# A decoder trunk whose order of instructions a planner makes: other planning rates, another order of two matmul groups, one scaling and two stores on other engines

## The chip, the cores and the metric

The kernel runs on one core of a Trainium2 chip. The metric is the time of one execution on the device in microseconds (us), lower is better. The core has five engines with queues of their own: TensorE (PE, with its weight loads shown apart as PEld), VectorE (DVE), ScalarE (ACT), GpSimd (POOL) and SyncE (SP, which only starts transfers). ACT and POOL can start transfers too. An engine works through its queue in order and waits at an instruction until its semaphores are reached.

## The reference, cut to what matters

Two decoder layers over 512 tokens of width 1024, 16 heads of 64, in float32.

```python
h = x
for layer in range(2):
    hn = rms_norm(h, attn_norm[layer])
    if layer == 0:   # mixer A: window 128, learned sinks, T5 bias
        h = h + swa_sink_mixer(hn, ...)
    else:            # mixer B: compressed, selected and windowed keys, gated
        h = h + nsa_mixer(hn, ...)
    h = h + swiglu(rms_norm(h, ffn_norm[layer]), w_gu[layer], w_down[layer])
return rms_norm(h, final_norm)
```

In mixer A each head's row of exponentials is divided by its sum (which includes the sink) before it meets the values: `p = e / (sum(e) + exp(sink - m))`. The feed-forward part is `(silu(gate) * up) @ w_down` with an inner width of 2816.

## The kernel before, in words

**Precision.** Every float32 operand is held as two halves, a rounded high part and the rest as a low part, so a product is three matmuls: high weight by high and by low data, low weight by high data (`step3`, line 614). The halves of weights are made on the chip from the loaded `raw` tile: either ACT rounds and DVE subtracts (`halves`), or, in `halves_by_dma` (line 589), one engine writes the negated rounded weights to `wlo` and a POOL transfer adds the weights from memory to it. With `aside=True` POOL does the rounding itself.

**Stages, with their times in the profile.** Loads, first norm and the keys and values of layer 0 (0 to about 25 us); attention A (to about 113); output projection A (to about 160); the plain part of feed-forward 0 (to about 239); its seven-product part (`seven`, line 1058, a Strassen-like scheme over 256 columns, to 480); the last down projection; projections of layer 1 (520 to 580); attention B (580 to 740); output projection B; feed-forward 1 in the same form (seven products from 860 to 1098); last down projection, final norm and stores.

**What sets the order.** The code does not issue instructions as it stands. Each call is recorded (`method`, line 202; `add`, line 210) with a cost and, for a transfer, a number of bytes and an extra delay `late`. Because the recorded calls are made from one lambda, nearly every instruction in the profile stands on line 207, and the tiles' names tell what it is. `issue` (line 274) then plans all engines together: for each of three pairs of transfer rate and latency in `SPEEDS` (line 58) it makes 6 rounds; in each, `plan` (line 423) is a list scheduler that gives an order, `latest` (line 311) works backwards from its end and gives each instruction a due time for the next round, and `replay` (line 360) plays that order 6 times with costs raised at random by up to 5% on all engines but PE and with the rates of `SPEEDS` in turn. The order with the lowest mean over the replays is issued. Every engine's queue is fixed by it, and so is the tile buffer that each instruction gets.

**The places that the change touches.**
- Small loads on ACT: `gains` (line 713), `rel_table` into `tab` (line 720) and two pieces of `onehot` into `oh` (line 725). In `add` a transfer that ACT starts has `late` 900.
- `project` (line 625) issues the 16 matmuls with the high weights first and the 8 with the low weights last. `query_job` (line 885) and `out_first_half` (line 892) use `mm3` (line 621), which takes the three of each slice in turn. They make the queries of the later head groups and the first part of the output projection; PE does them between the attention's own matmuls, in the one bank `mm`.
- Attention A has 16 units (4 head groups by 4 query blocks, `unit`, line 1248). In a unit PE makes the scores `S`, DVE adds the bias and takes the minimum (`pa`, `nm`), ACT takes the exponentials and sums (`sm`), `norm` (line 1289) inverts the sums on DVE and scales the four heads: head 0 on DVE, heads 1 to 3 on POOL. PE then transposes the scaled heads (`PT`), ACT and DVE split them (`ptp`), and PE multiplies with the values (`O`).
- At the end `last_down` (line 925) stores the second half of the tokens by 4 transfers `out_second` from tiles `fin`, all started by SP (line 975). ACT makes the two `fin` with m = 0, DVE the two with m = 1.

Of the kernel before, what the change touches and what calls it, by code (L numbers as in the profile page):

```python
# [55 lines left out]
ROUNDS = 6  # L56

SPEEDS = ((337.0, 1480.0), (310.0, 1650.0), (285.0, 1850.0))

TRIALS, NOISE = 6, 0.05  # L60
ENGINES = ("sp", "pe", "act", "dve", "pool")
# [101 lines left out]
class Scheduler:  # L163
# [46 lines left out]
    def add(self, name, m, call, writes, reads, args, kw):  # L210
        op = Op()
        op.eng, op.call, op.preds, op.succs, op.bytes, op.table, op.late = name, call, {}, [], 0, 0, 0.0
        op.prio = len(self.ops) + self.offset
        n = int(np.prod([c for _, c in writes[0].ap][1:]))
        psum = any("PSUM" in str(x.space) for x in writes + reads)
        parts = writes[0].ap[0][1]

        rows = sum(int(np.prod([c for _, c in x.ap][1:])) > 1 and "PSUM" not in str(x.space) for x in reads)

        if name == "pool":  # L220
            op.port = 1 if rows else 2
        else:
            op.port = 0 if name != "dve" else 1 if rows > 1 else 2 if (
                rows == 1 and not psum and m in ("tensor_scalar", "tensor_copy")) else 0
        if name == "pe":
            f4 = 1 if m == "transpose" or "float32r" in str(reads[0].dtype) else 4
            op.cost = max(n * f4 * 0.449 + 4.5, 109.0)
        elif m == "dma_start" and name != "pool":

            op.bytes = (7.2 if writes[0].tensor.name.startswith("biasA") else 4) * int(  # L230
                np.prod([c for _, c in writes[0].ap])) + 25000
            op.cost, op.late = (475.0, 0.0) if name == "sp" else (330.0, 900.0)
        elif name == "act":
            extra = sum(isinstance(kw.get(k), bass.AP) for k in ("bias", "scale", "accum_out"))
            op.cost = n * 0.83 + 93.0 * (1 + extra) - (40.0 if psum else 0.0) + (118.0 if parts == DH else 0.0)
            if m == "activation":
                op.table = self.TABLE.get(args[2].name, 0)
        elif name == "dve":
            if m == "reciprocal":
                op.cost = n * 6.2 + 65.0  # L240
            elif m == "tensor_reduce":
                op.cost = int(np.prod([c for _, c in reads[0].ap][1:])) * 1.04 + 130.0
            elif m == "memset" or (m in ("tensor_scalar", "tensor_copy") and not psum):
                op.cost = n * 0.52 + 130.0 + 80.0 * (len(args) > 2 and isinstance(args[2], bass.AP))
            else:
                op.cost = n * 1.04 + 70.0 + (60.0 if m == "scalar_tensor_tensor" else 0.0) + (
                    110.0 if parts < P and n > 100 else 0.0) + (63.0 if isinstance(kw.get("scalar"), bass.AP) else 0.0)
        elif name == "pool":
            if m == "dma_start":

                op.bytes = 6.6 * int(np.prod([c for _, c in writes[0].ap])) + 25000
                op.cost, op.port, op.late = 620.0, 2, 900.0
            elif m == "tensor_tensor":
                op.cost = n * 2.1 + 150.0
            else:
                op.cost = n * 0.83 + 162.0 + 82.0 * sum(isinstance(x, bass.AP) for x in args[2:4])
        op.tiles = {}
        for aps, write in ((writes, True), (reads, False)):
            for ap in aps:
                t, box = self.region(ap)  # L260
                past = self.seen.setdefault(t, ([], []))
                for w in (0, 1) if write else (0,):
                    for o, q in past[w]:
                        if o is not op and q[0] < box[1] and box[0] < q[1] and q[2] < box[3] and box[2] < q[3]:
                            op.preds[o] = True
                if t in self.tiles:
                    op.tiles[t] = True
        for aps, w in ((writes, 0), (reads, 1)):
            for ap in aps:
                t, box = self.region(ap)  # L270
                self.seen[t][w].append((op, box))
        self.ops.append(op)

    def issue(self):


        ops = self.ops
        for i, op in enumerate(ops):
            op.index = i
            op.succs = []  # L280
        for op in ops:
            for p in op.preds:
                p.succs.append(op)
        for op in ops:
            op.after = [(q.index, self.lag(op, q)) for q in op.succs]
        best = None
        for speed in SPEEDS:
            self.rate, self.latency = speed
            for op in ops:
                op.span = op.cost + (op.bytes / self.rate + self.latency + op.late if op.bytes else 0.0)  # L290
            far = {}
            for op in reversed(ops):
                far[op] = op.span + max((far[q] + (0.0 if q.eng == op.eng else 150.0) for q in op.succs), default=0.0)
            prio = [op.prio * PLACE - far[op] for op in ops]
            for _ in range(ROUNDS):
                self.rate, self.latency = speed
                span, order, start, given = self.plan(prio)
                prio = self.latest(start, span, given)
                mean = 0.0
                for trial in range(TRIALS):  # L300
                    self.rate, self.latency = SPEEDS[trial % len(SPEEDS)]
                    mean += self.replay(order, given, trial) / TRIALS
                if best is None or mean < best[0]:
                    best = mean, order
        for op in best[1]:
            op.call()
# [116 lines left out]
    def plan(self, prio):  # L423
# [74 lines left out]
        while left:  # L498
# [12 lines left out]
            while again:  # L511
                again = False
                for e in rules.engines(now):
# [21 lines left out]
                        heapq.heappush(ready[e], item)  # L535
                    if op is None:
                        continue
                    again, cost = True, rules.cost(op, now, 1.0)
                    if op.table and op.table != table:
                        table, cost = op.table, cost + TABLE_LOAD  # L540
                    start[i] = now
# [14 lines left out]
def trunk(ctx, tc, a, out):  # L556
# [64 lines left out]
    def mm3(o, w, x, n=P):  # L621
        for k in range(len(x)):
            step3(o, w, x[k], k, k == 0, k == len(x) - 1, n=n)

    def project(src, x, n=P, tag="S", by_dma=False):
        w = weights(src, cols=KT * n, by_dma=by_dma)
        p = bank(tag)

        line = [(k, 0, xi) for k in range(KT) for xi in range(2)] + [(k, 1, 0) for k in range(KT)]
        for m, (k, wi, xi) in enumerate(line):  # L630
            pe.matmul(p[:n], w[wi][:, k * n:(k + 1) * n], x[k][xi], start=m == 0, stop=m == len(line) - 1)
        return p


# [250 lines left out]
    def query_job(src, x, rstd, qs, tag, bias=None):  # L885

        w = weights(src, aside=True, by_dma=True)
        p = bank("mm")
        mm3(p, w, x)
        qs += query_pair(p, rstd, tag, bias=bias)  # L890

    def out_first_half(w, x, n, src, bias=None):

        for k in range(KT):
            h[k] = operand(f"h{n}_{k}", dtype=F32)
            sp.dma_start(h[k], src[k])
        for k in range(KT):
            ws = weights(w[k][:, :WOK * P], cols=WOK * P, aside=True, by_dma=True)
            p = bank("mm")
            mm3(p, ws, x[:WOK])  # L900
            if bias is None:
                dve.tensor_tensor(h[k], p, h[k], ALU.add)
            else:
                dve.scalar_tensor_tensor(h[k], p, bias[:, k:k + 1], h[k], op0=ALU.add, op1=ALU.add)
# [20 lines left out]
    def last_down(hid, w):  # L925

        kept, n = [], len(hid)
        for half in range(2):
# [35 lines left out]
            else:  # L964
                for j in range(2):
                    for m in range(2):
                        p = bank(("S", "S", "S", "mm")[2 * j + m])
                        for k in range(4):
                            pe.transpose(p[:, k * P:(k + 1) * P], h[4 * m + k][:, c][:, j * P:(j + 1) * P], ident)
                        o = operand("fin", dtype=F32)  # L970
                        if m:
                            dve.tensor_scalar(o, p, y[:, j:j + 1], None, op0=ALU.mult)
                        else:
                            act.activation(o, p, AF.Copy, scale=y[:, j:j + 1])
                        sp.dma_start(out[1][j * P:(j + 1) * P, m * T:(m + 1) * T], o)

    def keep(src, n, k):

# [269 lines left out]
    def unit(gq, i):  # L1248
# [40 lines left out]
        def norm():  # L1289
            dve.reciprocal(U.sm, U.sm)  # L1290
            for hh in range(4):
                (pool if hh else dve).tensor_scalar(
                    U.pp[hh][:, :nk], U.pp[hh][:, :nk], U.sm[:, hh:hh + 1], 1.0, op0=ALU.mult, op1=ALU.mult)

        def finish():
# [422 lines left out]
```

## Time and profile before

| | |
|---|---|
| runs shown | 1146.31, 1148.87, 1149.06 us; median 1148.87 |
| the profiled execution's own time | 1144.06 us |
| its span, first to last instruction | 1142.3 us |
| mean granted TensorE clock | 0.997 of full speed |
| busy: PE, DVE, ACT, POOL | 98%, 78%, 66%, 31% of the span |
| moved by transfers | 172.52 MB, 151 GB/s over the span |

In the rows below a time is in microseconds from the start of the span unless it is marked ns. A row of a window shows, for each engine, the busy time in it and in brackets the number of instructions; then the granted TensorE clock as a share of full speed (1.00 is 2.4 GHz, 0.50 is 1.2 GHz), the busy share of the 16 transfer engines and the rate in GB/s. A row of a wait says which engine, before which tile, waited for whom: total, times, longest. A row of the order of time is start, duration, engine, operation with output and inputs, shape, and in brackets the engine's idle time before it with what ended it. Matmuls overlap, so the duration of one says less than the number that starts in a window.

### The profile page before, as it was taken

What the parts mean: (1) busy time and instruction counts of PE and PEld (TensorE: products, weight loads), DVE (VectorE), ACT (ScalarE), POOL (GpSimd) and SP (SyncE); (2) the same over time, 40 slices, a digit from 0 to 9 for tenths busy, and PEclk for the clock granted to TensorE, in tenths of its full rate; (3) what the DMA queues carried; (4) which work ended last, traced back from release to release, by engine and by line L of the source; (5) the groups of instructions that cost most, each with busy time, mean ns of one, the idle gap of its engine ahead of it and who ended that gap; (6) DMA issues with size and microseconds to landing.
All of it is one profiled execution on the core that took longest, in us unless ns stands there. A gap on an engine that the chain in (4) does not pass through costs nothing.

```text
span 1142.3 us, 20667 instructions
## 1 busy us (share of the span) xinstructions
PE 1120.5 (98%) x7347; PEld 1001.2 (88%) x7347; DVE 895.1 (78%) x2039; ACT 749.3 (66%) x1539; POOL 356.2 (31%) x537
## 2 busy tenths in 40 slices
PE   8998999999999999999999999999999999999997
PEld 5887788899999999987878888877889999999997
DVE  6898568569888878776898989956948898988864
ACT  6777369367766757554577888838737766776763
POOL 3576821011121122000366866962001111122101
PEclk9999999999999999999999999999999999999999
DMA  7756548387788788853644215145748778779742
GB/s 215 189 112 152 111 120 198 84 201 183 156 206 190 153 176 194 242 187 101 186 110 102 56 39 148 31 108 146 169 109 198 173 169 220 172 164 208 180 110 75
DMA packets 65711, 172.52 MB, mean 151 GB/s; under 512 B 7910, under 2 KB 16358, under 8 KB 65608
## 3 DMA queue, kind: packets, MB, share of 16 engines
q0 software_dynamic: 21312, 58.73, 31.0%
q1 hardware_dynamic: 43376, 111.79, 30.5%
q8 instruction: 58, 0.95, 0.3%
q10 hardware_dynamic: 920, 0.68, 0.2%
q14 instruction: 45, 0.37, 0.1%
HBM read 166.39 MB, written 4.26 MB: 149 GB/s over the span
## 4 chain that ended last, share of the span: by engine, by line
PE 85%; DVE 7%; DMA 4%; ACT 2%; issue 1%; POOL 0%; ACTq 0%; DVEq 0%; SPq 0%
PE S L207 24%; PE Z L207 17%; PE X L207 16%; PE mm L207 10%; PE O L207 7%; PE Y L207 5%; PE PT L207 4%; DMA raw<-in_ffn_down 1%; DVE pa L207 1%; DVE wlo L207 1%; DMA raw<-in_ffn_gu 1%; DVE qsa L207 1%; DMA raw<-in_a_w_qkv 1%; DVE ptp L207 1%; DVE klb L207 1%
## 5 line engine op out<-in xcount | busy, mean ns | idle before, releaser
L207 ACT CAST whi<-s 128x512 fp32r<-128x512 f32 (+1 forms) x208 | 116.0, 584 | 64.2 <-PE X L207 38.2
L207 POOL DMA_DIRECT2D wlo<-in_ffn_gu x52 | 45.0, 866 | 358.5 <-ACT wlo L207 191.8
L207 DVE TENSOR_TENSOR wlo<-s,whi 128x512 fp32r<-128x512 f32 (+1 forms) x208 | 129.2, 645 | 31.1 <-ACT whi L207 30.5
L207 ACT CAST whi<-raw 128x1024 fp32r<-128x1024 f32 (+3 forms) x120 | 109.6, 915 | 57.3 <-PE S L207 25.6
L207 PE MATMUL Z<-xform,whi 128*128 128x256 f32 x864 | 130.2, 284 | 0.4 <-ACT rv L207 0.3
L207 PE MATMUL X<-xform,whi 128*128 128x256 f32 x864 | 127.1, 281 | 0.1
L207 PEld LDWEIGHTS Z<-xform,whi 128*128 128x128 f32 x864 | 114.1, 189 | 2.9 <-ACT rv L207 1.2
L207 PEld LDWEIGHTS X<-xform,whi 128*128 128x128 f32 x864 | 112.8, 189 | 0.6 <-DVE c L207 0.3
L207 ACT CAST ptp<-PT 128x512 fp32r<-128x512 f32 x108 | 61.5, 581 | 41.2 <-PE PT L207 35.0
L207 PE MATMUL S<-xl,whi 128*128 128x512 f32 (+1 forms) x216 | 86.5, 403 | 0.5 <-DVE xl L207 0.5
L207 PE MATMUL S<-xh,whi 128*128 128x512 f32 (+1 forms) x216 | 86.8, 406 | 0.0
L207 DVE TENSOR_TENSOR ptp<-PT,ptp 128x512 fp32r<-128x512 f32 x108 | 72.5, 686 | 13.4 <-ACT ptp L207 12.5
L207 DVE TENSOR_TENSOR s<-raw 128x512 f32<-128x512 f32 (+1 forms) x104 | 67.1, 645 | 17.9 <-DMA raw<-in_ffn_gu 10.2
L207 ACT ACTIVATE pb<-pb,nmb 128x128 f32<-128x128 f32 (+3 forms) x128 | 70.9, 556 | 10.5 <-DVE nmb L207 9.5
L207 POOL TENSOR_SCALAR pb<-pb,smb,gates 128x128 f32<-128x128 f32 (+3 forms) x120 | 71.7, 617 | 11.8 <-DVE smb L207 8.9
L207 PE MATMUL X<-xform,wlo 128*128 128x256 f32 x432 | 74.4, 281 | 0.0
L207 PE MATMUL Z<-xform,wlo 128*128 128x256 f32 x432 | 68.9, 281 | 0.0
L207 ACT ACTIVATE wlo<-raw 128x1024 fp32r<-128x1024 f32 (+1 forms) x68 | 68.3, 1005 | 0.7 <-PE S L207 0.6
L207 PE MATMUL O<-ptp,vb 128*128 128x512 f32 x160 | 64.4, 436 | 0.0
L207 PE MATMUL S<-xh,wlo 128*128 128x512 f32 x208 | 62.4, 402 | 0.1
L207 PEld LDWEIGHTS X<-xform,wlo 128*128 128x128 f32 x432 | 61.6, 190 | 0.0
L207 DVE CUSTOM_DVE_ANT_0 pb<-S,bias 128x128 f32<-128x128 f32 (+3 forms) x128 | 58.8, 481 | 3.4 <-PE S L207 2.8
(529 smaller groups left out, 3291.4 us busy)
## 6 DMA issues: line engine op xcount, KB each, us to landing
raw<-in_ffn_gu SPq DMA_DIRECT2D x88, 512.0 KB, 4.7
wlo<-in_ffn_gu POOLq DMA_DIRECT2D x52, 512.0 KB, 6.0
raw<-in_ffn_down SPq DMA_DIRECT2D x48, 384.0 KB, 4.1
w22l<-in_ffn_gu POOLq DMA_DIRECT2D x36, 256.0 KB, 5.0
raw<-in_b_w_in SPq DMA_DIRECT2D x14, 512.0 KB, 4.0
wlo<-in_ffn_down POOLq DMA_DIRECT2D x16, 384.0 KB, 5.1
raw<-in_a_w_qkv SPq DMA_DIRECT2D x9, 512.0 KB, 7.1
h<-in_x SPq DMA_DIRECT2D x16, 256.0 KB, 4.3
```

The costliest lines, as they stand in the source:

```text
L207: self.add(name, m, lambda: getattr(eng, m)(*args, **kw), writes, reads, args, kw)
```

## The change: what it does

- `PLANS` replaces `SPEEDS` in `issue`: three pairs of rate and latency, each with a factor `margin` by which `plan` raises the costs of all engines but PE. The replays still use `SPEEDS` and their random costs.
- A transfer that ACT starts, other than those to 64 partitions, has `late` 3300 in place of 900: the small loads at the start and, by the last edit, two stores.
- `query_job` and `out_first_half` take the order that `project` has, by a new function `mm3_late`.
- In attention A head 0 is scaled on POOL, like the other three.
- The `out_second` stores with m = 0 are started by ACT, those with m = 1 by SP.

```diff
@@ -56,6 +56,8 @@
 SPEEDS = ((337.0, 1480.0), (310.0, 1650.0), (285.0, 1850.0))
+
+PLANS = (((285.0, 1850.0), 1.04), ((270.0, 2000.0), 1.02), ((300.0, 1700.0), 1.03))
@@ -229,7 +231,7 @@
-            op.cost, op.late = (475.0, 0.0) if name == "sp" else (330.0, 900.0)
+            op.cost, op.late = (475.0, 0.0) if name == "sp" else (330.0, 900.0 if parts == DH else 3300.0)
@@ -284,7 +286,7 @@
-        for speed in SPEEDS:
+        for speed, self.margin in PLANS:
             self.rate, self.latency = speed
@@ -535,7 +537,7 @@
-                    again, cost = True, rules.cost(op, now, 1.0)
+                    again, cost = True, rules.cost(op, now, self.margin)
@@ -622,13 +624,16 @@
+    def mm3_late(o, w, x, n=P):
+
+        line = [(k, 0, xi) for k in range(len(x)) for xi in range(2)] + [(k, 1, 0) for k in range(len(x))]
+        for m, (k, wi, xi) in enumerate(line):
+            pe.matmul(o, w[wi][:, k * n:(k + 1) * n], x[k][xi], start=m == 0, stop=m == len(line) - 1)
+
     def project(src, x, n=P, tag="S", by_dma=False):
         w = weights(src, cols=KT * n, by_dma=by_dma)
         p = bank(tag)
-
-        line = [(k, 0, xi) for k in range(KT) for xi in range(2)] + [(k, 1, 0) for k in range(KT)]
-        for m, (k, wi, xi) in enumerate(line):
-            pe.matmul(p[:n], w[wi][:, k * n:(k + 1) * n], x[k][xi], start=m == 0, stop=m == len(line) - 1)
+        mm3_late(p[:n], w, x, n)
         return p
@@ -886,7 +891,7 @@
-        mm3(p, w, x)
+        mm3_late(p, w, x)
@@ -897,7 +902,7 @@
-            mm3(p, ws, x[:WOK])
+            mm3_late(p, ws, x[:WOK])
@@ -972,7 +977,7 @@
-                        sp.dma_start(out[1][j * P:(j + 1) * P, m * T:(m + 1) * T], o)
+                        (sp if m else act).dma_start(out[1][j * P:(j + 1) * P, m * T:(m + 1) * T], o)
@@ -1289,7 +1294,7 @@
-                (pool if hh else dve).tensor_scalar(
+                pool.tensor_scalar(
```

## Rows read from the trace of the kernel before

**Rows 1.** The page, busy time of PE: us (share of the span), instructions.

```profile
PE 1120.5 (98%) x7347; PEld 1001.2 (88%) x7347; DVE 895.1 (78%) x2039; ACT 749.3 (66%) x1539; POOL 356.2 (31%) x537
```

**Rows 2.** Windows by stage: start, attention A, its end, projections and attention B.

```profile
0.00:25.00 25.00, 20.55 (x72) 13.75 (x73) 17.26 (x36) 16.34 (x30) 6.29 (x22) 1.00 0.69 223
...
40.00:100.00 60.00, 58.66 (x327) 48.29 (x326) 55.77 (x169) 47.17 (x135) 39.88 (x73) 1.00 0.57 141
100.00:120.00 20.00, 16.43 (x87) 13.29 (x86) 18.04 (x54) 11.27 (x35) 13.32 (x25) 0.91 0.34 80
...
520.00:580.00 60.00, 56.77 (x293) 45.77 (x292) 45.37 (x75) 28.81 (x46) 15.71 (x16) 1.00 0.56 154
580.00:740.00 160.00, 159.53 (x925) 130.94 (x926) 143.63 (x564) 134.30 (x383) 117.84 (x203) 1.00 0.28 71
```

**Rows 3.** Order of time at the start, ACT and its queue; copies of the bias row.

```profile
0.75 0.62 ACTq L207 DMA_DIRECT2D oh<-in_onehot  x1
...
1.78 0.43 ACTq L207 DMA_DIRECT2D gains<-in_gains  x1
...
6.14 0.72 ACT L207 ACTIVATE xh<-h,gains 128x512 fp32r<-128x512 f32 x1 [1.45 <-DMA gains<-in_gains]
...
15.10 1.04 ACT L207 COPY row<-prv 16x512 f32<-16x512 f32 x2
```

**Rows 4.** Chain that ended last, at the start: start, us, what.

```profile
1.78 4.27 DMA gains<-in_gains
```

**Rows 5.** The scalings of attention A by tile: ns min/median/max, first and last start.

```profile
L207 POOL TENSOR_SCALAR pa<-pa,sm x48: 362/482/798, 45.7 to 127.5; 128x256 f32<-128x256 f32 x36, 128x128 f32<-128x128 f32 x12
...
L207 DVE TENSOR_SCALAR pa<-pa,sm x16: 281/538/1440, 45.6 to 121.6; 128x256 f32<-128x256 f32 x12, 128x128 f32<-128x128 f32 x4
```

**Rows 6.** Waits from 25 to 125 us.

```profile
POOL pa L207 <- DVE sm L207: 20.1, 6, 7.3
...
PE S L207 <- DVE nm L207: 2.3, 1, 2.3
```

**Rows 7.** Windows around the longest wait of PE in attention A.

```profile
25.00:113.00 88.00, 84.08 (x457) 68.89 (x455) 77.40 (x207) 61.28 (x162) 55.54 (x95) 1.00 0.64 153
111.00:114.00 3.00, 0.66 (x4) 0.46 (x4) 2.92 (x14) 2.46 (x11) 1.08 (x2) 1.00 0.00 0
...
115.00:119.00 4.00, 3.58 (x12) 2.98 (x13) 3.34 (x13) 2.09 (x10) 4.00 (x8) 0.57 0.00 0
```

**Rows 8.** DVE from 25 to 113 us: count, busy us, mean ns, idle before; durations of qsa.

```profile
L207 DVE SCALAR_TENSOR_TENSOR qsa<-ev,bq,qsa 64x512 fp32r<-64x512 f32 x16 | 15.3, 957 | 2.0 <-ACT qsa L207 1.6
...
L207 DVE TENSOR_SCALAR pa<-pa,sm 128x256 f32<-128x256 f32 (+1 forms) x12 | 6.6, 574 | 0.1
...
L207 DVE SCALAR_TENSOR_TENSOR qsa<-ev,bq,qsa x16: 745/762/1884, 35.1 to 107.8; 64x512 fp32r<-64x512 f32 x16
```

**Rows 9.** Waits of PE from 25 to 155 us, those before the bank mm.

```profile
PE mm L207 <- DVE ev L207: 1.1, 2, 0.8
...
PE mm L207 <- POOL oa_0l L207: 0.4, 1, 0.4
```

**Rows 10.** Windows of the seven-product parts of feed-forward 0 and 1.

```profile
238.78:480.48 241.70, 239.87 (x1996) 237.43 (x1996) 198.93 (x383) 163.56 (x304) 43.70 (x51) 1.00 0.81 186
859.94:1097.83 237.89, 237.89 (x1997) 237.01 (x1997) 198.56 (x374) 164.75 (x305) 43.28 (x50) 1.00 0.80 183
```

**Rows 11.** Chain in feed-forward 0, from 300 to 460 us: first and last of five transfers.

```profile
312.77 4.77 DMA raw<-in_ffn_down
...
422.13 5.28 DMA raw<-in_ffn_gu
```

**Rows 12.** The last stores and DVE's last tile; transfers in the window after them.

```profile
1136.97 1.91 SPq L207 DMA_DIRECT2D out_second<-fin  x4
1136.98 0.74 DVE L207 TENSOR_SCALAR fin<-mm,y 128x512 f32<-128x512 f32 x1
...
1138.00:1139.00 1.00, 0.00 (x0) 0.00 (x0) 0.00 (x0) 0.00 (x0) 0.00 (x0) 1.00 1.04 401
```

## The prediction

> **What bounds the kernel now.** First the page's busy times: PE is busy for 1120.5 of 1142.3 us [rows 1], so all its gaps together are 21.8 us. No part of the change takes work from PE: the two matmul groups that get another order keep their number. What can be won is gaps, and matmuls that wait unseen inside busy time. Second, the windows by stage, for where these lie [rows 2]. The start has 25.00 - 20.55 = 4.45 us of gaps. Attention A has 1.34 in its 40 to 100 us and 3.57 in the 20 us after, with a lower clock there; DVE is busy for 55.77 of 60 there, 93%, and for 18.04 of the next 20. The projections of layer 1 have 3.23. Attention B has 0.47, with DVE at 143.63 of 160, so it is near both limits. Third, the two seven-product parts, the same work twice, show what hides in busy time: 1996 matmuls in 241.70 us in layer 0, 1997 in 237.89 in layer 1 [rows 10]. That is 3.8 us, though PE shows only 1.83 of gaps in the slower. The chain names the cause: five transfers of weights of some 5 us lie on it in layer 0 (first and last in [rows 11]). Last, the end: after DVE's last tile only stores run [rows 12].
>
> **Scaling of head 0 on POOL.** 16 DVE instructions go, with a median of 538 ns and a minimum of 281 [rows 5]. 12 of them lie between 25 and 113 us and hold DVE for 6.6 us [rows 8], of 77.40 busy in 88 [rows 7]. POOL gets 16 more at its 482 ns [rows 5], 7.7 us; it is busy for 55.54 of 88 [rows 7] and waits 20.1 us in 6 places for the sums that DVE inverts, just ahead of these scalings [rows 6], so it has room. Behind them in its queue stand the roundings and the adding transfers of the next query weights, and the copies of the sinks that ACT's next exponentials need. In a unit the four heads now pass POOL one after another, so the last head comes 0.48 us later than before; other units' work on PE hides that while there is any. If that cover is gone, it costs 16 x 0.48 = 7.7 us. The gain is a stall: PE waits 2.34 us for DVE's minimum before 113.5 us (2.3 in [rows 6]), and DVE is busy for 2.92 of the 3 us around it [rows 7]. 6.6 us less of DVE ahead of that place can remove all of it. Then the clock: from 115 to 119 us the mean granted is 0.57 [rows 7], so about 0.86 of those 4 us are at 1.2 GHz, which costs half of 3.4, 1.7 us, and it comes after the stall. So the most that A can give is 1.34 + 3.57 + 1.7 = 6.6 us, the least is minus 7.7. I take the stall alone, **-2.3**; the clock may fall at another gap. Late next would be the outputs that POOL splits for the projection (PE waited 0.4 for them, [rows 9]).
>
> **High weights first in queries and first half of the projection.** 28 groups (6 + 6 of queries, 8 + 8 of the projections) keep their matmuls; only the wait for `wlo` moves to the last third. PE's waits before the bank `mm` in A are for DVE, which frees the single bank, 1.1 us, and for POOL's split, 0.4 [rows 9]; none is for `wlo`. So the new order frees no wait that shows. The planner may start a group earlier, which then holds the only bank longer. I take **0**, between -1.5 (both waits gone) and +1.1 (DVE's wait for the bank doubled).
>
> **Small loads at the start.** The chain runs through the load of the gains, started at 1.78 us and 4.27 long [rows 4]; ACT's first scaling at 6.14 waited 1.45 for it [rows 3]. A planner that counts 2400 ns more for these loads should start first what the longest chain needs. If the gains take the slot at 0.75 [rows 3] they come 1.03 us sooner. At most 1.45 is won, when ACT waits for nothing; at worst the table that is moved behind pushes ACT's two copies of the bias row, 1.04 us [rows 3], into the chain. I take **-1.0**, between -1.45 and +1.0. SP's own queue isn't touched by this edit.
>
> **Two queues for the last stores.** SP's four starts take 1.91 us from 1136.97, so the last ends at 1138.88; DVE's last tile is ready at 1137.72 [rows 12]. With two on ACT, SP's last start can follow that tile at once, and end 0.4 later (a start is 0.33 to 0.62 on ACT, [rows 3]): up to 0.8 sooner. But from 1138 us the transfer engines are full, at 1.04 and 401 GB/s [rows 12], so what remains is the earlier filling. I take **-0.3**, between -0.8 and +0.4 (ACT's start stands ahead of its second tile).
>
> **Other rates and a margin.** The planner counted a transfer at up to 337 bytes a ns; now at most 300, and other engines 2 to 4% slower, so it puts loads further ahead and believes in less overlap. What that can repair is the 3.8 us of feed-forward 0 [rows 10, 11]. But the slowest old pair is the fastest but one of the new ones, and layer 1 was planned by the same rules without a loss. A fresh plan loses in one such part or in none or both. I take half, **-1.9**, between -3.8 and +3.8 (layer 1 gets layer 0's loss). Attention B and the projections before it I take at 0, between -3.2 and +3.2, the gaps of 520 to 580 us gone or doubled [rows 2].
>
> **Sum.** -2.3 + 0 - 1.0 - 0.3 - 1.9 = -5.5 us. The profiled execution's own time is 1144.06, 1.8 over its span; it becomes 1138.6. The median of the runs, 1148.87, stands 4.8 above that execution, and I forecast on the median: 1143.4. From no change a measurement of this kernel can tell about 0.3%, 3.4 us; the three runs spread over 2.75.
>
> **Rivals.**
> *Only the ends move.* PE is at 98%, and DVE's freed time in A goes to other waits: -1.3 gives 1147.6. For it: attention A's gaps are few and each has another releaser. Against: the longest has DVE busy beside it. Also here belongs that the planner leaves the loads where they were and finds much the same order: 1148.9. Together 0.18.
>
> *POOL blocks DVE.* What leaves DVE's queue comes back as waiting inside other DVE instructions. The rows show such waiting now: the DVE instruction that makes `qsa` takes 745 ns at least and 957 in the mean over 16 [rows 8], 3.4 us in all, and the removed scalings 574 against 281 [rows 5, 8]. If each of the added 12 POOL scalings in the stage blocks DVE for its length, 12 x 0.48 = 5.8 of the 6.6 us come back; the stall stays, and -3.2 gives 1145.7. The Trainium skill ("SBUF — State Buffer", section "Who interferes with whom") states that a DVE instruction with two SBUF inputs contends with a GpSimd instruction that reads SBUF, and that the loser blocks for the whole instruction; it speaks against this edit, and the spread of `qsa`, which reads two, agrees with it. The same section lets scalings on DVE contend too, and their spread agrees as well. That is why I don't take the full return: the edit removes one blocker where it adds another, and the two-input kind has lost 3.4 us beside 55.54 of POOL's work, so 5.8 more would add some 0.4. Chance 0.10.
>
> *POOL becomes late in attention A, slower.* Place: the last of the four scalings in a unit, ahead of PE's transposes. Price: 0.48 in each of 16 units, 7.7, less 1.3 for the ends and 1.9 for the feed-forward: +4.5, so 1153.4. It decides where POOL's 20.1 us of waiting for the sums [rows 6] are used up and PE's waits end on POOL instead of DVE. Against: POOL is busy for 63% of the stage, 72% with the 7.7. Chance 0.11.
>
> *The new plan misses where the old one hit, slower.* Feed-forward 1 gets the 3.8 and the gaps before attention B double, 3.2, with nothing won in A: 7.0 - 1.3 = +5.7, so 1154.6. For it: a plan is chosen by replays, and layer 0 shows that a chosen plan can be late on transfers. Against: the new rates are slower, so loads should be early. Chance 0.09.
>
> **Numbers.** Forecast 0.52, with a range of its own from 1137 (ends of start, A, feed-forward 0 and stores: -1.45 - 6.6 - 3.8 - 0.8 = -12.6) to 1145.4. Only the ends, and blocking, 0.28, lie within 0.3%. The two slower cases have 0.20. The range of 1137 to 1153 leaves out about 0.04 below and 0.13 above. So faster 0.52, same 0.28, slower 0.20.
>
> **What would show it.** Right: the wait of PE on `nm` near 113 us gone, and 100 to 120 at a clock of 1.00; `gains` first on ACT's queue and the first `xh` near 5.1; feed-forward 0 in some 240 us; `out_second` on ACT and SP, the last start before 1138.5 relative to the same DVE end; DVE's `pa` scalings gone and POOL's 64. Wrong: waits of `PT` on POOL in A, `qsa` well over 957 ns, transfers on the chain in feed-forward 1, or more gaps between 520 and 740 us.

## The result, and the profile after

The changed kernel takes 1136.95 us (median of 6 runs, 1134.48 to 1138.61) against 1148.96 (6 runs, 1146.31 to 1152.07): a ratio of 0.9894, 95% interval 0.9873 to 0.9915. That is 12.0 us less, where 5.5 was forecast. The profiled execution took 1136.71 us with a span of 1134.9, so between the two profiled executions only 7.35 us lie; the other 4.7 are the distance of the old median from the old profiled execution, which the new kernel doesn't have.

The page's busy line of the changed kernel, for [rows 1], and its windows of the start, attention A, its end, the projections of layer 1 and attention B, for [rows 2]:

```profile
PE 1115.1 (98%) x7347; PEld 1003.5 (88%) x7347; DVE 888.5 (78%) x2023; ACT 751.0 (66%) x1539; POOL 361.9 (32%) x553
```

```profile
0.00:25.00 25.00, 21.33 (x84) 15.76 (x85) 16.98 (x36) 16.30 (x30) 9.00 (x24) 0.90 0.75 241
40.00:100.00 60.00, 57.15 (x319) 48.05 (x318) 51.45 (x155) 45.54 (x131) 40.34 (x79) 0.92 0.54 141
100.00:120.00 20.00, 18.40 (x96) 15.44 (x95) 16.84 (x56) 14.14 (x46) 17.51 (x34) 0.87 0.30 59
520.00:580.00 60.00, 57.65 (x305) 47.03 (x304) 47.50 (x107) 32.91 (x69) 17.84 (x21) 0.95 0.59 165
580.00:740.00 160.00, 159.25 (x927) 132.50 (x926) 143.76 (x533) 133.05 (x366) 117.97 (x201) 0.98 0.30 72
```

More matmuls start in the first 25 us (84 for 72) and in the 60 of the projections (305 for 293), fewer in attention A up to 100 us (319 for 327). The clock of 0.95 that runs through this execution to 657 us stands at 1.00 in the second execution of the same kernel, whose span is 1135.1, so nothing is explained by it. Where the 7.35 us lie is seen when both traces are cut at the same matmuls:

| from one matmul to the next, us | before | after | difference |
|---|---|---|---|
| span's start to the first of the queries of A (`S<-kha,qsa`) | 37.85 | 35.50 | -2.35 |
| to the last of the output projection A (`S<-oa`) | 128.56 | 128.74 | +0.18 |
| to the last of the seven products of layer 0 | 313.78 | 312.07 | -1.71 |
| to the first of the queries of B (`S<-khb,qsb`) | 97.30 | 96.31 | -0.99 |
| to the last of the output projection B (`S<-ob`) | 209.98 | 209.21 | -0.77 |
| to the last of the seven products of layer 1 | 310.09 | 308.52 | -1.57 |
| to the end | 44.73 | 44.59 | -0.14 |

**Start.** ACT's four loads stand in the same order and at the same times; the first `xh` starts at 6.12 for 6.14 [rows 3]. SP's queue changed: the first piece of weights now goes ahead of `x`. The rows are SP's first transfer and PE's first matmul of the projection, before and after:

```profile
0.75 0.38 SPq L207 DMA_DIRECT2D h<-in_x  x1
...
9.14 0.79 PE L207 MATMUL S<-xh,whi 128*128 128x512 f32 x1
```

```profile
0.75 0.38 SPq L209 DMA_DIRECT2D raw<-in_a_w_qkv  x1
...
6.89 0.50 PE L209 MATMUL S<-xh,whi 128*128 128x512 f32 x1 [1.20 <-ACT xh L209]
```

**Attention A.** The waits of PE from 25 to 125 us, for [rows 6], the tile rows of the scalings and of `qsa`, for [rows 5, 8], and two windows, for [rows 7]:

```profile
PE PT L209 <- DVE ptp L209: 2.2, 2, 2.1
PE S L209 <- DVE qsa L209: 2.2, 3, 1.0
```

```profile
L209 POOL TENSOR_SCALAR pa<-pa,sm x64: 362/476/983, 44.4 to 125.6; 128x256 f32<-128x256 f32 x48, 128x128 f32<-128x128 f32 x16
...
L209 DVE SCALAR_TENSOR_TENSOR qsa<-ev,bq,qsa x16: 736/750/4218, 33.2 to 110.1; 64x512 fp32r<-64x512 f32 x16
```

```profile
83.00:87.00 4.00, 3.84 (x17) 3.14 (x16) 3.84 (x6) 1.16 (x2) 0.00 (x0) 0.57 0.60 98
110.50:114.50 4.00, 3.50 (x17) 3.44 (x18) 3.97 (x23) 3.03 (x14) 3.90 (x4) 0.57 0.18 34
```

The wait of 2.3 us for the minima is gone. In its place one `qsa` on DVE took 4218 ns, where 736 is the least, PE waited 2.1 us for `ptp` behind it, and there are two stretches at the lower clock where there was one. It is the same in the two other profiles of the changed kernel (4255 and 4229 ns). Beside this `qsa` POOL splits outputs, rounds weights and copies sinks, and scales no head (order of time, rows from 79.5 us on).

```profile
77.52 4.22 DVE L209 SCALAR_TENSOR_TENSOR qsa<-ev,bq,qsa 64x512 fp32r<-64x512 f32 x1
79.17 1.00 POOL L209 TENSOR_SCALAR whi<-raw 128x768 fp32r<-128x768 f32 x1
...
80.22 0.98 POOL L209 TENSOR_SCALAR wlo<-raw 128x768 fp32r<-128x768 f32 x1
```

**Feed-forward and stores.** Windows of the seven-product part of layer 0, from its first matmul to its last, in both kernels (the sizes of the stretch are the point, 2035 matmuls in each):

```profile
231.69:480.19 248.50, 246.67 (x2035) 243.38 (x2035) 203.67 (x390) 166.32 (x309) 44.27 (x52) 1.00 0.81 185
```

```profile
229.58:476.31 246.73, 245.43 (x2035) 242.97 (x2034) 203.69 (x392) 168.62 (x309) 44.99 (x53) 0.95 0.83 187
```

The stores, for [rows 12]: two on each queue, and the last one starts at 1130.5, as DVE's last tile is done; before, with all four on SP, it started at 1138.5, some 0.8 after that tile. Yet from PE's last matmul to the end 6.39 us pass, for 6.52 before.

```profile
L209 ACTq DMA_DIRECT2D out_second<-fin x2: 369/388/406, 1129.8 to 1130.3; - x2
L209 SPq DMA_DIRECT2D out_second<-fin x2: 332/332/332, 1129.9 to 1130.5; - x2
```

### The profile page after: what moved, and what is told of

Same layout as the page of the kernel before. It is cut to its first block, busy times and chain, and to the rows that moved or that the text cites. A ratio compares the mean times of both kernels' runs of the same rounds, so it can differ in the third digit from the quotient of the medians.

```text
span 1134.9 us, 20662 instructions
## 1 busy us (share of the span) xinstructions
PE 1115.1 (98%) x7347; PEld 1003.5 (88%) x7347; DVE 888.5 (78%) x2023; ACT 751.0 (66%) x1539; POOL 361.9 (32%) x553
## 4 chain that ended last, share of the span: by engine, by line
PE 88%; DVE 5%; DMA 3%; ACT 2%; issue 1%; POOL 1%; ACTq 0%; DVEq 0%; POOLq 0%; SPq 0%
PE S L209 25%; PE Z L209 17%; PE X L209 17%; PE mm L209 10%; PE O L209 7%; PE Y L209 5%; PE PT L209 4%; DMA raw<-in_ffn_down 1%; DVE qsa L209 1%; PE psq L209 1%; DMA wlo<-in_ffn_gu 1%; DVE wlo L209 1%; DVE ptp L209 1%; PE pc L209 0%; DVE ev L209 0%
## 5 line engine op out<-in xcount | busy, mean ns | idle before, releaser
L209 ACT CAST whi<-s 128x512 fp32r<-128x512 f32 (+1 forms) x208 | 118.5, 585 | 73.2 <-PE X L209 48.6
L209 DVE TENSOR_TENSOR wlo<-raw,whi 128x1024 fp32r<-128x1024 f32 (+3 forms) x52 | 49.2, 949 | 17.4 <-ACT whi L209 15.9
```

What stands on the lines that cost most here:

```text
L209: self.add(name, m, lambda: getattr(eng, m)(*args, **kw), writes, reads, args, kw)
```

## The experiments

Three theories stood against each other: the planning brings the gain (its rates, or its margin), the local parts bring it, or any new plan lands somewhere. All ratios are to the kernel before in the same rounds.

**A second execution of the kernel before** (no edit).

> The kernel before, unchanged, profiled a second time. Its profiled execution had an own time of 1144.06 us, its six timed runs 1146.31 to 1152.07, median 1148.96. Theory 1 (the forecast was taken from an execution that is about 5 us faster than usual): the second profile has an own time of 1147 to 1152, and the extra lies in some stage that the first profile shows without it. Theory 2 (a profiled execution is faster than a timed one, whatever the kernel): again about 1144.

Measured 1151.59 us. Up to attention B the two executions agree within 0.6 us; attention B to its output projection takes 214.00 for 209.98, the seven products of layer 1 248.25 for 244.20 (the windows of both, first execution, then second):

```profile
577.49:787.47 209.98, 208.02 (x1163) 169.65 (x1162) 173.76 (x613) 157.41 (x422) 142.19 (x236) 1.00 0.34 83
853.36:1097.56 244.20, 244.20 (x2034) 242.58 (x2032) 203.75 (x381) 167.75 (x310) 44.14 (x51) 1.00 0.80 183
```

```profile
576.93:790.93 214.00, 209.51 (x1162) 170.96 (x1161) 176.28 (x613) 157.32 (x422) 141.47 (x236) 0.99 0.33 82
856.83:1105.08 248.25, 246.18 (x2033) 244.10 (x2032) 203.67 (x381) 167.57 (x310) 44.03 (x51) 0.99 0.77 180
```

The order of time of this second execution shows what lies behind the first of these two differences, around 732 us:

```profile
731.32 4.21 POOL L207 TENSOR_SCALAR pb<-pb,smb,gates 128x384 f32<-128x384 f32 x6
...
731.96 3.84 DVE L207 TENSOR_SCALAR pb<-pb,smb,gates 128x512 f32<-128x512 f32 x1
...
736.45 0.34 PE L207 MATMUL PT<-ident,pb 128*128 128x128 f32 x1 [2.57 <-DVE ptp L207]
```

A scaling on DVE that takes 546 ns in the median stood from just before the second of six POOL scalings in a row to just behind their end; PE ran dry for 2.57 us, and the window after shows the lower clock. Behind the second difference is a late transfer, and the same follows. Windows, then the chain:

```profile
737.00:740.00 3.00, 3.00 (x12) 2.51 (x11) 1.52 (x3) 1.17 (x2) 0.90 (x1) 0.50 0.46 54
866.00:870.00 4.00, 2.15 (x18) 1.95 (x17) 1.70 (x3) 1.75 (x4) 0.83 (x1) 0.97 0.67 132
870.00:873.50 3.50, 3.50 (x19) 3.50 (x19) 2.99 (x6) 1.07 (x3) 0.03 (x1) 0.55 0.71 132
```

```profile
861.68 6.54 DMA raw<-in_ffn_gu
```

So one order has executions some 8 us apart, and the one that I read was a lucky one: of the 88 timed runs of the kernel before in all rounds, from 1141.85 to 1155.34 us, 6 are at or below its 1144.06. The changed kernel has neither gap in its three profiles: attention B takes 209.01 to 209.25 us, the seven products of layer 1 242.93 to 243.84, and its 14 timed runs lie between 1133.56 and 1138.61.

**The two halves of the change.** `plans_only` has `PLANS`, the loop over it and `self.margin`; `all_but_plans` has everything else.

```diff
-        for speed in SPEEDS:
+        for speed, self.margin in PLANS:
...
-                    again, cost = True, rules.cost(op, now, 1.0)
+                    again, cost = True, rules.cost(op, now, self.margin)
```

> The kernel before with the three new pairs of rates and the margins alone; all other parts of the change undone. Theory P (the planning rates and margins bring the gain): 1137 to 1141 us, a ratio of 0.988 to 0.993 to the kernel before, with feed-forward 0 near 240 us. Theory L (the local parts bring it: POOL's scalings, high weights first, late small loads, two queues for the stores): 1147 to 1151, ratio 0.998 to 1.002. Theory N (every new plan lands somewhere, whatever its rule): anything from 1135 to 1155, with the gain or loss in stages that no edit touches.

> The changed kernel with the old rates and no margin in the planning; all other parts of the change as they are. Theory P: 1146 to 1151 us, ratio 0.998 to 1.002. Theory L: 1137 to 1141, ratio 0.988 to 0.993. Theory N: anything from 1135 to 1155, and the sum of this change and of the one with the plans alone is not the whole change's minus 12.

Measured: plans alone 1145.07 us, ratio 0.9959 (0.9936 to 0.9982); all but plans 1147.73, 0.9987 (0.9969 to 1.0006). Without the plans the local parts bring nothing that can be told apart; the plans alone bring a part.

**Rates or margin.** Only the numbers of `PLANS` differ: margin with the old rates, new rates with all margins at 1.0.

```diff
+PLANS = (((337.0, 1480.0), 1.04), ((310.0, 1650.0), 1.02), ((285.0, 1850.0), 1.03))
```

> The kernel before with the three old pairs of rates and with margins of 1.04, 1.02 and 1.03 on them; nothing else. Theory M (the margin is what counts in the new plans, since it leaves the other engines room ahead of PE): 1140 to 1146, ratio 0.992 to 0.997, as plans_only or better. Theory R (the slower rates count): 1147 to 1151, ratio 0.998 to 1.002.

> The kernel before with the three new pairs of rates and all margins at 1.0; nothing else. Theory R: 1140 to 1146, ratio 0.992 to 0.997. Theory M: 1147 to 1151, ratio 0.998 to 1.002.

Measured: margin alone 1142.04, 0.9946 (0.9920 to 0.9972); rates alone 1147.40, 0.9996 (0.9966 to 1.0026). In the total the margin is what counts. By stage the profiles, one of each order, divide it otherwise: attention A with its projection takes 127.05 us with the margin alone and 127.90 with the rates alone (128.56 before), attention B 207.49 and 214.60 (209.98), but the seven products of layer 0 take 249.21 with the margin alone and 247.05 with the rates alone (248.50). Of all orders run here, the four with the old rates take 248.15 to 250.07 us for this part, seven of the eight with the new rates 244.35 to 247.10, and one 249.08. The profile of the rates alone has the blocked scaling of attention B, 3912 ns; that of the margin alone has none over 1131 ns in either attention.

**Late loads alone.**

```diff
+            op.cost, op.late = (475.0, 0.0) if name == "sp" else (330.0, 900.0 if parts == DH else 3300.0)
```

> The kernel before with the extra delay of 3300 for the transfers that ACT starts; nothing else. The four ACT loads stand in the same order in the changed kernel, but the plan around them starts PE's first projection 2.2 us earlier. If that is this edit's: the first matmul of the first projection before 7 us, the first query matmul of attention near 36 us in place of 37.9, and some 2 us less in all (1147.5). If the plan beyond the start decides (theory N), the start is better and the total anything from 1142 to 1153.

Measured 1147.10, 0.9994 (0.9970 to 1.0018). The first matmul of the projection starts at 6.29 us and the first query matmul at 35.68, for 9.14 and 37.85: the earlier start is this edit's. In all orders that were planned with the edit the first query matmul starts between 34.68 and 36.47 us, in those without it between 36.89 and 41.01. It doesn't reach the end: the profile has another wait for DVE of 3.2 us in the projections of layer 1, and a DVE scaling of 3843 ns in attention B.

**The scaling with the order held.** Both kernels issue the planned order word for word and send head 0's scaling to the other engine; the second also sends ACT's two stores back to SP.

```diff
+            on = self.on or eng
-            self.add(name, m, lambda: getattr(eng, m)(*args, **kw), writes, reads, args, kw)
+            self.add(name, m, lambda: getattr(on, m)(*args, **kw), writes, reads, args, kw)
```

> The order of the kernel before, instruction by instruction, but head 0 of attention A is scaled on POOL when it is issued. This is my step of minus 2.3 us by itself. If that step holds: the wait of PE on the minima near 113 us gone, the clock at full speed there, and 2.3 to 4 us less (1144.5 to 1146.5). Rival, POOL blocks DVE: what leaves DVE's queue comes back in its two-input instructions, their longest over 3000 ns in place of 1884, attention A as long as before within 1 us (1147.5 to 1149.5). Rival, POOL late in A: up to 7.7 us more (1152 to 1157).

> The order that the planner gives to the changed kernel, instruction by instruction, but when it is issued head 0 is scaled on DVE and all four last stores are started by SP. This is the direct cost of those two edits with the order held. If freeing DVE in attention A is worth something of its own (my step: 2.3 us) and the two queues 0.3: 1139.6 us or up to 1143. If only the order counts: 1136 to 1138, the same as the changed kernel.

Measured: POOL in the old order 1153.28, 1.0036 (1.0016 to 1.0057), slower; DVE in the new order, with all stores on SP, 1143.27, 0.9938 (0.9909 to 0.9966), some 6 us over the changed kernel. In the old order with POOL, attention A with its projection takes 131.51 us, where the two executions of the kernel before have 128.56 and 128.41. (The profile is of the slowest of the ten runs, 1158.85, so only this stage is read from it.) The wait for the minima stays, one `qsa` takes 2881 ns, beside roundings of weights on POOL, and PE now waits for POOL as well (waits from 25 us on, then `qsa`):

```profile
PE S L208 <- DVE nm L208: 2.3, 1, 2.3
PE PT L208 <- POOL pa L208: 2.0, 2, 1.7
```

```profile
L208 DVE SCALAR_TENSOR_TENSOR qsa<-ev,bq,qsa x16: 745/750/2881, 35.9 to 111.5; 64x512 fp32r<-64x512 f32 x16
```

Of the three theories the slower one, POOL late in attention A (1152 to 1157), fits the total. In the new order with DVE, attention A with its projection takes 135.80 us for 128.74, and the long `qsa` is there all the same:

```profile
L210 DVE SCALAR_TENSOR_TENSOR qsa<-ev,bq,qsa x16: 733/750/3964, 34.0 to 116.9; 64x512 fp32r<-64x512 f32 x16
```

Either swap costs: an order fits the engines that it was made for.

**The scaling with a new plan.** Each is the changed kernel with one edit: the first undoes the line in `norm`, the second sends attention B's last DVE scalings to POOL too, the third adds a pair to `PLANS`.

```diff
-                pool.tensor_scalar(
+                (pool if hh else dve).tensor_scalar(
...
-                (dve if i == hh == 3 else pool).tensor_scalar(
+                pool.tensor_scalar(
...
+PLANS = (((285.0, 1850.0), 1.02), ((285.0, 1850.0), 1.04), ((270.0, 2000.0), 1.02), ((300.0, 1700.0), 1.03))
```

> The changed kernel planned anew with head 0 of attention A on DVE; all else as changed. If the scaling on POOL is worth something once the plan is made for it: 1140 to 1145 us, ratio 0.992 to 0.997. If it is worth nothing: 1136 to 1139. In both cases the stages from 165 us on should be as in the changed kernel within 2 us; if they differ by more, the new plan and not the scaling is what is measured.

> The changed kernel with the last four DVE scalings of each branch of attention B (one head of the last query block, 8 in all) on POOL too. In two profiles of old plans one of these took 3.84 and 3.91 us, since it stood behind six POOL scalings in a row, and opened a gap of PE of some 2.6 us with 3.41 us at half clock. If that blocking also hits the changed kernel in some executions: 1133 to 1136.5 us, and the shortest execution no shorter than the changed kernel's 1134.5 by more than 1 us. If its order avoids it already: 1136 to 1139. If POOL becomes the late one in B: 1139 or more.

> The changed kernel with a fourth pair among the plans, 285 and 1850 with a margin of 1.02. If a smaller margin that still leaves room gives a better order: 1130 to 1135 us, ratio 0.984 to 0.989. If every plan with a margin lands in the same few us: 1135 to 1139. If the margin has to be at least 3% to protect against blocked instructions and late transfers: 1139 to 1145, with a spread of its runs as wide as that of the kernel before.

Measured: head 0 on DVE 1137.92, 0.9905 (0.9872 to 0.9939); B's scalings on POOL too 1139.75, 0.9923 (0.9893 to 0.9952); the fourth pair 1136.63, 0.9907 (0.9878 to 0.9935), its runs from 1133.89 to 1143.56. With head 0 on DVE, attention A with its projection takes 128.61 us, in the three profiles of the changed kernel 127.86 to 129.30: the POOL scaling is worth nothing that shows once the plan is made for it. The total alone wouldn't say so, since feed-forward 0 differs by more than the 2 us that were set (314.24 for 312.07). With B's scalings on POOL nothing is won, and attention B takes 210.73 us for 209.21; no scaling blocks there in the changed kernel, whose longest is 1408, 1497 and 1475 ns in three profiles. The fourth pair gives the same median, with wider runs.

**What the margin needs beside it.** New plans with the late loads, and new plans with the high weights first; then the first again with the plans alone and the changed kernel on one chip. The changed kernel was also run beside the margin kernels.

> The kernel before with the new rates and margins and with the delay of 3300 for ACT's transfers; two matmul groups, scaling and stores as before. Plans alone gave 1145.1, plans with late loads, late low weights and two queues 1137.9. Theory D (the plans alone lose at the start what the delay gives back: first query matmul of attention at 40.7 us with the plans alone, 37.9 before, 34.9 to 35.5 with the delay): 1138 to 1141.5. Theory W (the order of the matmul groups gives the room, by letting high weights run while the low ones are on their way): 1143 to 1147.

> The kernel before with the new rates and margins and with high weights first in the queries and the first half of the projection; loads' delay, scaling and stores as before. Theory D: 1143 to 1147. Theory W: 1138 to 1141.5. If neither of the two comes under 1142, the rest of the gain needs both, or is the luck of the plan.

> The kernel with new plans and the loads' delay alone, a second time, beside the changed kernel on one chip. If it is better than the whole change (plan without the POOL scaling): 1131 to 1134 us, some 4 us under the changed kernel in the same rounds. If that was the first chip's: within 1.5 us of it.

> The kernel with the new plans alone, a second time. If its order is worse than that of plans_late by itself (a start later by 4 us, one DVE scaling blocked for 3.8 us): 1142 to 1147 again, its profile with a blocked instruction or a late start. If it was the chip: 1133 to 1139.

> The changed kernel, a third time. 1135 to 1138 us. If the chip sets the difference between the runs of the other calls, it moves with the two others beside it.

> The changed kernel, unchanged, on the chip and in the rounds of the three runs beside it. Theory S (the executions of a kernel spread by some 8 us, since a late transfer or a blocked DVE instruction opens a gap that also drops the clock; the changed order has more room and shows fewer): median 1135 to 1140, ratio 0.988 to 0.992, and a second profile that differs from the first by a few us at single places, in attention and feed-forward. Theory C (the first chip was kind): 1141 or more.

| kernel | median us (lowest to highest) | ratio (95% interval) |
|---|---|---|
| plans and late loads | 1132.61 (1130.81 to 1133.76) | 0.9846 (0.9790 to 0.9901) |
| plans and high weights first | 1135.68 (1131.67 to 1136.63) | 0.9866 (0.9817 to 0.9914) |
| plans and late loads, again | 1133.09 (1132.16 to 1135.85) | 0.9863 (0.9812 to 0.9914) |
| plans alone, again | 1145.52 (1140.12 to 1149.24) | 0.9974 (0.9947 to 1.0001) |
| changed kernel, beside the two above | 1135.02 (1133.56 to 1136.49) | 0.9873 (0.9830 to 0.9916) |
| changed kernel, beside the margin kernels | 1136.82 (1136.54 to 1137.21) | 0.9912 (0.9883 to 0.9941) |

Both of the first two came in lower than either theory had them, so neither theory is borne out. It is the order and not the chip. With the plans alone the first query matmul of A starts at 40.73 and 41.01 us, with the late loads at 36.33 and 35.61; from it to the last of output projection A 128.81 and 129.34 us pass, against 125.33 in both. So the start holds 4.4 and 5.4 us of the difference and attention A 3.5 and 4.0, together 7.9 of the 8.7 us between the first two spans (1138.9 and 1130.2) and 9.4 of the 11.7 between the second two (1142.7 and 1131.0). In both profiles of the plans alone one scaling is blocked, and neither of the others has that (the tile row, first execution):

```profile
L209 DVE TENSOR_SCALAR pa<-pa,sm x16: 282/465/3846, 54.1 to 125.9; 128x256 f32<-128x256 f32 x12, 128x128 f32<-128x128 f32 x4
```

And the best kernel shows no lower clock where the others lose theirs (its windows of attention A, A's end, and the end of attention B):

```profile
40.00:112.00 72.00, 69.51 (x390) 57.04 (x388) 65.69 (x201) 53.37 (x155) 50.36 (x89) 1.00 0.55 137
112.00:120.00 8.00, 7.87 (x43) 6.33 (x42) 7.14 (x26) 6.12 (x24) 7.29 (x14) 1.00 0.30 55
720.00:745.00 25.00, 25.00 (x136) 19.87 (x135) 16.83 (x44) 12.43 (x27) 15.12 (x24) 1.00 0.34 68
```

Plans and late loads alone are as fast as the whole change or faster: 1133.09 against 1135.02 in the same rounds, where the two kernels' runs overlap; the 1.9 us lie between the two expectations.

All orders together speak for the margin. The four that were planned without one (the kernel before, the local parts, the rates, the late loads) have medians of 1147.10 to 1149.57 us, the eight with one 1132.61 to 1145.52. In attention B the profiles without a margin show 209.38 to 214.60 us; those with one 206.95 to 209.25, and 210.73 where all of B's scalings are on POOL. How much of it an order gets, within 13 us, is the third theory's share.

## Why the prediction was wrong, by its steps

**The base of the sum failed.** "The median of the runs, 1148.87, stands 4.8 above that execution, and I forecast on the median": I took the 4.8 as a constant that both kernels have. On its own execution the sum gave 1138.6, and 1136.71 was measured; on the median it gave 1143.4, and 1136.95 was measured. The second profile of the kernel before shows that such a distance is made of gaps that open in some executions: a blocked DVE scaling and a late transfer, each followed by a stretch at 1.2 GHz. The changed kernel's profiles have neither, so the distance is part of what the change removes: 4.7 of the 6.5 us between the change that was forecast, 5.5, and the one that was measured, 12.0. The margin by itself doesn't remove it: with the plans alone the runs spread from 1140.12 to 1152.91, and the profiled one stands 4.4 below their median. The three runs shown, all above the profiled one, hinted that it was a lucky one. The lower end of the range fails too: its terms, -12.65 from 1148.87, give 1136.2 and not 1137, and 1136.95 lies between the two.

**Other rates and a margin, -1.9: right where it was put, but the margin's gain elsewhere was taken at nothing.** In the profiled executions feed-forward 0 gained 1.8 us (248.50 to 246.73), as forecast, and with the rates alone it gains 1.45. Why it does isn't shown. The five transfers on the chain, which the prediction names as the cause, are not it: in the second execution of the kernel before two lie there, and the part takes 248.15. But feed-forward 1, the projections and attention B gained too, together 3.3, where I took 0 ("Attention B and the projections before it I take at 0"). I argued from the rates, which bring nothing in the total (0.9996); the margin does (0.9946), and its profile gains where I had put nothing, in attention B (207.49 for 209.98) and in attention A (127.05 for 128.56).

**Scaling on POOL, -2.3: wrong.** Stage A with its projection took 128.56 us before and 128.74 after. The stall that I wanted to remove did go, but not because DVE had less to do: in the old order with head 0 on POOL it stays at 2.3 us, and in the new order with head 0 on DVE it is 0.3. The order removes it. In the old order the edit has the other sign, 131.51 us for 128.56: PE waits for POOL's scalings, 2.0 us, the rival *POOL becomes late* in its place but not at its price of 7.7. The rival *POOL blocks DVE* named the instruction that would wait, `qsa`, and was right that the stage would win nothing, but not on what blocks it: the long ones stand beside POOL's roundings and splits, and the longest of the new order takes 3964 ns with head 0 on DVE, where 4218 with it on POOL. So it belongs to the order and not to the scaling. I had weighed that rival down to 0.4 us by spreading the waiting evenly over POOL's time; it comes in single events. (The 574 against 281 there also compares two shapes: 281 is a scaling of 128x128, and the least of 128x256 is 353.) Planned anew the edit is worth nothing that shows (1137.92 without it).

**Small loads, -1.0: right in direction, wrong in mechanism.** 2.35 us came, more than the 1.45 that I gave as the most. That bound held only for the gains, which did not move. "SP's own queue isn't touched by this edit" was the step that failed: the planner, told that ACT's loads land late, put SP's first weights ahead of `x`, and PE's first matmul started 2.25 us earlier. That matmul alone doesn't carry the gain: in the second execution of the kernel before it starts 0.92 us earlier (8.22), and the first query matmul at 37.97. How the rest builds up in between isn't shown.

**High weights first, 0.** The waits of PE before the bank `mm`, 1.1 and 0.4 [rows 9], are gone in the changed kernel, but they are gone with the plans alone too, so this edit isn't what removes them. Together with the margin it gives a much better order than the plans alone (1135.68 for 1145.07), and so does the late load. So the 0 holds for the edit by itself only as far as [rows 9] show it; it was never run alone. Which of the planner's choices makes the better order isn't shown; shown is where the difference lies, at the start and in attention A.

**Stores, -0.3:** -0.14 in the profile. The filled transfer engines [rows 12] left little to win: after the change they are at 1.03 and 1.04 from 1131 to 1133 us.

Of the other rivals, the POOL queue became the late one in the old order (PE waits of 2.0 us on `pa`, 1.0036) but not in the changed kernel; feed-forward 1 did not lose.

## What to carry to other kernels

A profiled execution is one draw: where timed runs lie apart from it by more than the change is worth, look for what differs between executions before a sum is made on it, and count rare gaps at their mean. In a fixed order for all engines a blocked instruction or a late transfer can become a gap of PE, 2.57 us long in the case above. A few per cent on the other engines' costs were worth more here than moving work between engines. That they work by leaving room for such events is my reading and not shown: the planner already counts that DVE and POOL hold each other up and that PE is slower behind gaps (`Rules`, methods `held` and `cost`), and whether it had counted the long waits above isn't shown. A single part of such a change cannot be valued by the order that it happens to give: here the same plans gave 1133 to 1146 us with one small edit more or less.

## What the runs showed of the hardware that was not expected

A DVE instruction beside GpSimd can take as long as a whole run of GpSimd instructions, not only as long as one: 3840, 3912, 3843 and 3866 ns in four profiles of orders without a margin, at the same scaling of attention B whose median is some 546 to 616, and 1267 in the first profile of the same order as the first of these. The Trainium skill ("SBUF — State Buffer", section "Who interferes with whom") states of the port pair that the two share that, against a DVE instruction in a two-port mode, whoever issues first gets it for the whole instruction and the other blocks; in which mode this scaling ran no row shows. The trace agrees that DVE waits, but it did so through five further GpSimd instructions (731.96 to 735.80 us beside six scalings from 731.32).

A short gap of PE costs more than its length. In the second execution of the kernel before, attention B took 4.0 us more (214.00 for 209.98) with one gap of PE of 2.57 us, and the window behind that gap, 737 to 740 us, was granted 0.50, the lower of TensorE's two levels (1.2 GHz) throughout; behind the late transfer 0.55 was granted from 870 to 873.5 us.
